# Four of the first eight column blocks of a modulation, moved from VectorE to TensorE as four-byte products

## The chip, the cores and the metric

The kernel runs on one core of one Trainium2 chip. The metric is the time of one execution on the device, in microseconds (us). TensorE multiplies, VectorE and ScalarE (DVE and ACT in the profile) work elementwise, SyncE (SP) issues most of the transfers from memory, GpSimd (POOL) a few. TensorE's weight loads have a row of their own (PEld) and overlap its matmuls (PE).

## The reference, cut to what matters

Two transformer blocks run one after the other on 256 tokens of 1024 features. The first begins so:

```python
mod = c @ w_ada[l] + b_ada[l]                  # c: 1 x 1024, w_ada: 1024 x 3072
shift, scl, gate = jnp.split(mod, 3, axis=-1)
h = rms_norm(x, g_norm[l]) * (1.0 + scl[:, None, :]) + shift[:, None, :]
proj = h @ w_in[l]
```

The change touches `mod` of this first block alone. All values are four-byte floats.

## The kernel before, in words

**The modulation.** The host lays `w_ada` out as 24 column blocks of 128 columns, transposed: block i is a tile of 128 partitions (the columns) x 1024 (the inputs). Shift and scale blocks alternate: block 2k is the shift of features 128k to 128k + 127, block 2k + 1 their scale; the last eight are the gate. `ada` (L368) streams one block into a buffer `raw`, multiplies it with `c1b`, a copy of the condition on every partition, and sums along the row, in one VectorE instruction (L370, with a short read of the accumulator behind it). The result is one column of `mod1`.

**The first projection.** h is kept transposed, in eight blocks of 128 features x 256 tokens, each as two parts, `bh` (rounded) and `bl` (the rest), so that three fast matmuls stand for one exact product (`mm3`, L243 to L246). A loop over kk (L404 to L421) takes four blocks of the modulation at a time, adds the bias (`biased`, L373), forms `am` from the scales (L418) and then two blocks of h (`hT_block`: L330 and L332 on VectorE, L331 on ScalarE). Blocks 8 to 11 and 13 to 15 are each followed by half a projection tile (`proj_n`): its weights are streamed, cast (`whi`, L239, ScalarE), subtracted (`wlo`, L240, VectorE) and used in 24 matmuls of 256 columns. The first tile of weights is called tile 0 in what follows; it needs the first four blocks of h, so blocks 0 to 7.

**Ahead of it** ScalarE squares x, VectorE forms the reciprocal root `rstd` (L289 to L299), and TensorE transposes x in 16 pieces (L319) and spreads `rstd` to rows in a PSUM tile `rb` (L324) that L330 reads.

**What sets the order.** Each engine works its instructions in a fixed order that a scheduler made from the program; the fences below show it. `raw` has five buffers, which blocks and weight tiles share; SP issues a transfer when the buffer's last reader is done, in order. The order holds for whole tiles: a write to any part of a tile waits for its readers so far.

Of the kernel before, what the change touches and what calls it, by code (L numbers as in the profile page):

```python
# [7 lines left out]
F32 = mybir.dt.float32  # L8
# [88 lines left out]
def _pack(I):  # L97
    I = {k: np.asarray(v) for k, v in I.items()}
    A = {}
# [12 lines left out]
    tl = lambda v: v.reshape(-1, 128).T  # L112
# [3 lines left out]
    def inter(w):  # L116

        n = w.shape[-1] // 3072
        w = w.reshape(w.shape[:-1] + (n, 3, 8, 128))
        sc = np.stack([w[..., 0, :, :], w[..., 1, :, :]], axis=-2).reshape(w.shape[:-4] + (n, 2048))  # L120
        return np.concatenate([sc, w[..., 2, :, :].reshape(w.shape[:-4] + (n, 1024))], axis=-1).reshape(w.shape[:-4] + (-1,))
# [5 lines left out]
    A["bcmp"] = np.stack([I["b_cmp_k1_2"][0], I["b_cmp_v1_2"][0]])  # L127
    A["gfin"] = I["g_final"][None]
    A["gnf"] = I["g_norm_final_2"][None]
    A["wada1"] = inter(I["w_ada"][0]).T.reshape(24, 128, 1024)  # L130
    A["wada2"] = inter(I["w_ada_2"][0]).T.reshape(48, 128, 1024)
    w = I["w_in"][0]
    A["win1n"] = rows(cat(w[:, 1024:2560], w[:, 0:512]))
# [4 lines left out]
    w = I["w_in_2"][0]  # L138
# [5 lines left out]
    w = I["w_out_2"][0]  # L144
# [10 lines left out]
    return {k: np.ascontiguousarray(v) for k, v in A.items()}  # L155


VEC = {}
_o = 0
for _n, _w in (("b1", 24), ("g1", 8), ("ps", 4), ("b2", 48), ("gm", 8), ("gf", 8),  # L160
# [10 lines left out]
def _body(ctx, tc, ins, out, dbg, stop):  # L171
    nc = tc.nc
    V, S, G, T = nc.vector, nc.scalar, nc.gpsimd, nc.tensor
# [14 lines left out]
    def vcol(n, i=0, w=None):  # L188
        o, ww = VEC[n]
        return vec[:, o + i:o + i + (ww - i if w is None else w)]  # L190
# [14 lines left out]
    def bc_row(pool, ap, name, tag=None, q=S):  # L205
        t = pool.tile([128, 1024], F32, name=name, tag=tag or name)
        q.dma_start(t, bass.AP(tensor=ap.tensor, offset=ap.offset, ap=[[0, 128], [1, 1024]]))
        return t
# [16 lines left out]
    def stream(name, i):  # L225
        t = raw.tile([128, 1024], F32, name="raw")
        loaded[0] = nc.sync.dma_start(t, ins[name][i])
        return t
# [110 lines left out]
    with ExitStack() as c1:  # L339
        k1 = c1.enter_context(tc.tile_pool(name="k1", bufs=1))  # L340
# [10 lines left out]
        x_sb = k1.tile([128, 2, 1024], F32, name="x_sb")  # L351
        for t in range(2):
            S.dma_start(x_sb[:, t], ins["x"][t * 128:(t + 1) * 128])
        c1b = bc_row(k1, ins["c1"], "c1b", "tm1", nc.sync)
        load_consts(const, "ka")
        ident = K["ident"]
# [12 lines left out]
            for i in range(lo, hi):  # L369
                V.scalar_tensor_tensor(scr2, stream(name, i), 1.0, row, op0=OP.mult, op1=OP.mult, accum_out=mod[:, i:i + 1])  # L370

        def biased(mod, bias, lo, hi):
            V.tensor_add(mod[:, lo:hi], mod[:, lo:hi], vcol(bias, lo, hi - lo))  # L373


        mode[0] = "V"
# [13 lines left out]
        V.tensor_copy(mask, K["mask"])  # L390
        identb = k1.tile([128, 128], BF, name="identb")
        V.tensor_copy(identb, ident)
        rb = pov.tile([128, 256], F32, name="rb", tag="ov")
        for t in range(2):
            rows(rb[:, t * 128:(t + 1) * 128], rstd[:, t:t + 1])
        xT = xT_in(v_sb, u_sb)
# [7 lines left out]
        for kk in range(4):  # L404
            lo = 4 * kk
            for i in range(lo, lo + 4):
                if i > 1:
                    with tc.issue_after(ready.ins):
                        ada("wada1", mod1, c1b, "b1", i, i + 1)
                else:  # L410
                    ada("wada1", mod1, c1b, "b1", i, i + 1)
                for _ in range(begin.get(i, 0)):
                    n = len(first)
                    q, g = ((pmm, "mm"), (pmm, "mm"), (psc, "sc"), (psc, "sc"), (psc, "sc"), (ptr, "tp"), (ptr, "tp"))[n]
                    first.append(q.tile([128, 2, 256], F32, name="mm", tag=g))
                    proj_n(first[n], "win1n", n, *h1, (0,))
            biased(mod1, "b1", lo, lo + 4)
            V.scalar_tensor_tensor(am[:, 2 * kk:2 * kk + 2], mod1[:, lo + 1:lo + 4:2], 1.0, vcol("g1", 2 * kk, 2),  # L418
                                   op0=OP.add, op1=OP.mult)
            for k in (2 * kk, 2 * kk + 1):  # L420
                hT_block(*hT, k, xT, rb, am, lambda k: mod1[:, 2 * k:2 * k + 1], w1)  # L421
# [839 lines left out]
    for c in range(64, 124):  # L1261
        upc(G1, c)
        if c % 4 == 3 and 68 <= c < 100:
            i = 40 + (c - 68) // 4
# [49 lines left out]
```

## Time and profile before

| | us |
|---|---|
| three runs | 1246.6, 1245.26, 1244.03 |
| median | 1245.26 |
| profiled execution, its own time | 1246.62 |
| its span, first to last instruction | 1244.8 |

| stretch (us) | what runs there |
|---|---|
| 0 to 11 | transfers; ScalarE squares x |
| 11 to 16.5 | transposes of x and the rows of rstd on TensorE; VectorE: block 1, rstd, blocks 2 and 3 |
| 16.5 to 24.7 | VectorE: blocks 4 to 8 and the first two blocks of h; TensorE waits |
| 24.7 to 47 | first halves of seven projection tiles; VectorE: blocks 9 to 15, the other blocks of h, the low halves |
| from 47 on | TensorE busy nearly without pause to the end |

The times in the rows below count from the span's start. A timeline row is one instruction, or several like ones in a row (xN); behind it, in brackets, stands how long the engine had been idle and what ended that.

### The profile page before, as it was taken

Reading aid. Unit: us, or ns where it says so; the run is one execution under the profiler, and the core shown is the slowest. Engines: PE = TensorE matmul, PEld = TensorE weight load, DVE = VectorE, ACT = ScalarE, POOL = GpSimd, SP = SyncE. Lnnn points to the kernel's source line nnn. Section 1 sums busy time; section 2 is a strip of 40 time slices with the busy share of each in tenths; the row PEclk is TensorE's granted clock in tenths of the full one; section 3 lists DMA queues with packets and bytes.
Section 4 is the critical chain, followed back from the end, with each engine's and each line's share of the span. In section 5 each row is a group of like instructions: output and inputs, shape, how many; then the busy total and the mean of one; then the engine's idle time right before and its main releaser. Section 6 shows DMA issues by size and latency. Waiting matters only on the chain. (4 is left out here: it accounts for less than half of the span.)

```text
span 1244.8 us, 22791 instructions
## 1 busy us (share of the span) xinstructions
PE 1190.5 (96%) x8960; PEld 1071.1 (86%) x8960; DVE 959.2 (77%) x2015; ACT 585.6 (47%) x907; POOL 8.7 (1%) x14
## 2 busy tenths in 40 slices
PE   3999999899999899899999999999999999999996
PEld 2998899778788799899999999998777777888884
DVE  6879869768798789997546778778888887666555
ACT  3445547323553545454544444445444444555553
POOL 0000000000000000000000000000000000000001
PEclk9999999999999999999999999999999999999998
DMA  9999846287373444556565555555555556777551
GB/s 320 363 323 317 284 163 198 92 287 253 103 238 118 170 143 165 169 171 202 190 195 175 170 170 170 170 169 171 169 172 179 173 172 237 227 230 238 183 186 51
DMA packets 67451, 245.22 MB, mean 197 GB/s; under 512 B 7504, under 2 KB 8032, under 8 KB 67088
## 3 DMA queue, kind: packets, MB, share of 16 engines
q1 hardware_dynamic: 65136, 236.34, 57.7%
q10 hardware_dynamic: 1440, 4.20, 0.9%
q0 software_dynamic: 768, 3.23, 0.8%
q8 instruction: 70, 1.15, 0.4%
q14 instruction: 37, 0.30, 0.1%
HBM read 241.11 MB, written 2.62 MB: 196 GB/s over the span
## 5 line engine op out<-in xcount | busy, mean ns | idle before, releaser
L240 DVE TENSOR_TENSOR wlo<-raw,whi 128x1024 fp32r<-128x1024 f32 x351 | 427.9, 1222 | 121.8 <-ACT whi L239 120.7
L239 ACT CAST whi<-raw 128x1024 fp32r<-128x1024 f32 x351 | 368.0, 1050 | 326.4 <-PE pa L245 221.7
L246 PE MATMUL pa<-bh,wlo 128*128 128x256 f32 x1120 | 314.6, 281 | 3.7 <-DVE wlo L240 3.5
L244 PE MATMUL pa<-bh,whi 128*128 128x256 f32 x1120 | 317.2, 283 | 0.0
L245 PE MATMUL pa<-bl,whi 128*128 128x256 f32 x1120 | 313.9, 280 | 0.0
L246 PEld LDWEIGHTS pa<-bh,wlo 128*128 128x128 f32 x1120 | 211.7, 189 | 5.0 <-DVE wlo L240 4.9
L245 PEld LDWEIGHTS pa<-bl,whi 128*128 128x128 f32 x1120 | 214.5, 192 | 0.0
L244 PEld LDWEIGHTS pa<-bh,whi 128*128 128x128 f32 x1120 | 211.8, 189 | 0.0
L1219 PE MATMUL up<-whi,bh 128*128 128x512 f32 x508 | 164.1, 403 | 0.0
L1219 PE MATMUL up<-wlo,bh 128*128 128x512 f32 x508 | 160.1, 394 | 0.0
L1219 PE MATMUL up<-whi,bl 128*128 128x512 f32 x508 | 159.8, 394 | 0.0
L1219 PEld LDWEIGHTS up<-wlo,bh 128*128 128x128 f32 x508 | 95.4, 188 | 23.5 <-DVE wlo L240 0.3
L1219 PEld LDWEIGHTS up<-whi,bl 128*128 128x128 f32 x508 | 95.4, 188 | 22.3
L244 PE MATMUL mm<-whi,bh 128*128 128x256 f32 x352 | 102.2, 290 | 11.0 <-ACT whi L239 8.2
L1219 PEld LDWEIGHTS up<-whi,bh 128*128 128x128 f32 x508 | 93.4, 189 | 19.3 <-ACT whi L239 0.2
L245 PE MATMUL mm<-wlo,bh 128*128 128x256 f32 x352 | 101.2, 288 | 2.1 <-DVE wlo L240 2.1
L246 PE MATMUL mm<-whi,bl 128*128 128x256 f32 x352 | 101.1, 287 | 1.1 <-DVE bl L332 1.0
L1185 DVE TENSOR_TENSOR RL<-E,wpt 128x512 f16<-128x512 f16 x128 | 53.9, 422 | 33.7 <-PE tp L1199 33.7
L244 PEld LDWEIGHTS mm<-whi,bh 128*128 128x128 f32 x352 | 67.8, 193 | 13.1 <-ACT whi L239 8.6
L245 PEld LDWEIGHTS mm<-wlo,bh 128*128 128x128 f32 x352 | 67.7, 192 | 3.2 <-DVE wlo L240 2.5
L246 PEld LDWEIGHTS mm<-whi,bl 128*128 128x128 f32 x352 | 67.7, 192 | 2.3 <-DVE bl L332 1.7
L231 ACT CAST bh<-Ga 128x256 fp32r<-128x256 f32 x64 | 25.4, 406 | 86.3 <-PE up L1219 85.1
(400 smaller groups left out, 1709.7 us busy)
## 6 DMA issues: line engine op xcount, KB each, us to landing
raw<-in_wdT_dram SPq DMA_DIRECT2D x128, 512.0 KB, 3.4
raw<-in_wu_dram SPq DMA_DIRECT2D x128, 512.0 KB, 3.5
raw<-in_wada_dram SPq DMA_DIRECT2D x72, 512.0 KB, 4.8
raw<-in_win_dram SPq DMA_DIRECT2D x26, 512.0 KB, 4.5
raw<-in_win1t_dram SPq DMA_DIRECT2D x24, 512.0 KB, 5.0
raw<-in_win1n_dram SPq DMA_DIRECT2D x16, 512.0 KB, 5.2
raw<-in_wout_dram SPq DMA_DIRECT2D x16, 512.0 KB, 3.6
raw<-in_wq_dram SPq DMA_DIRECT2D x12, 512.0 KB, 3.6
```

The costliest lines, as they stand in the source:

```text
L231: S.copy(hi, src)
L239: S.copy(hi, t)
L240: (E or eng()).tensor_tensor(lo, t, hi, op=OP.subtract)
L244: T.matmul(o, a[0], b[0], start=first, stop=False, **kw)
L245: T.matmul(o, a[0], b[1], start=False, stop=False, **kw)
L246: T.matmul(o, a[1], b[0], start=False, stop=last, **kw)
L1185: V.tensor_tensor(L[:, p], E, pair(wpt[:, p], t).to_broadcast([128, ng // 2, 64, 2]), op=OP.mult)
L1219: T.matmul(up[t][d], s_[:, ts], v_[:, d], start=ia == 0 and n == 0, stop=ia == 127 and n == 2)
```

## The change

For blocks 0, 2, 4 and 6 (the shifts of the first four blocks of h) the host stores the weights untransposed, as eight pieces of 128 inputs x 128 columns side by side. `ada_t` multiplies each piece, as the stationary operand, with one column of `c1t` (the condition as 128 x 8, a new 4 KB transfer on POOL's queue), and adds the eight products up in one column of PSUM. The four columns lie behind `rb` in the same PSUM tile, now called `rbm`. `biased` adds the bias to the even columns from PSUM and to the odd ones from `mod1`, in two instructions instead of one.

```diff
@@ -127,7 +127,10 @@
     A["bcmp"] = np.stack([I["b_cmp_k1_2"][0], I["b_cmp_v1_2"][0]])
     A["gfin"] = I["g_final"][None]
     A["gnf"] = I["g_norm_final_2"][None]
-    A["wada1"] = inter(I["w_ada"][0]).T.reshape(24, 128, 1024)
+    A["wada1"] = inter(I["w_ada"][0]).T.reshape(24, 128, 1024).copy()
+    for i in ADA_T:
+        A["wada1"][i] = A["wada1"][i].T.reshape(8, 128, 128).transpose(1, 0, 2).reshape(128, 1024)
+    A["c1t"] = tl(I["c"][0])
     A["wada2"] = inter(I["w_ada_2"][0]).T.reshape(48, 128, 1024)
     w = I["w_in"][0]
     A["win1n"] = rows(cat(w[:, 1024:2560], w[:, 0:512]))
@@ -155,6 +158,7 @@
     return {k: np.ascontiguousarray(v) for k, v in A.items()}
 
 
+ADA_T = (0, 2, 4, 6)
 VEC = {}
 _o = 0
 for _n, _w in (("b1", 24), ("g1", 8), ("ps", 4), ("b2", 48), ("gm", 8), ("gf", 8),
@@ -351,6 +355,8 @@
         x_sb = k1.tile([128, 2, 1024], F32, name="x_sb")
         for t in range(2):
             S.dma_start(x_sb[:, t], ins["x"][t * 128:(t + 1) * 128])
+        c1t = k1.tile([128, 8], F32, name="c1t")
+        G.dma_start(c1t, ins["c1t"])
         c1b = bc_row(k1, ins["c1"], "c1b", "tm1", nc.sync)
         load_consts(const, "ka")
         ident = K["ident"]
@@ -369,8 +375,13 @@
             for i in range(lo, hi):
                 V.scalar_tensor_tensor(scr2, stream(name, i), 1.0, row, op0=OP.mult, op1=OP.mult, accum_out=mod[:, i:i + 1])
 
-        def biased(mod, bias, lo, hi):
-            V.tensor_add(mod[:, lo:hi], mod[:, lo:hi], vcol(bias, lo, hi - lo))
+        def ada_t(o, i):
+            w = stream("wada1", i)
+            for k in range(8):
+                T.matmul(o, w[:, k * 128:(k + 1) * 128], c1t[:, k:k + 1], start=k == 0, stop=k == 7, skip_group_check=True)
+
+        def biased(mod, bias, lo, hi, step=1, src=None):
+            V.tensor_add(mod[:, lo:hi:step], mod[:, lo:hi:step] if src is None else src, vcol(bias, lo, hi - lo)[:, ::step])
 
 
         mode[0] = "V"
@@ -390,7 +401,8 @@
         V.tensor_copy(mask, K["mask"])
         identb = k1.tile([128, 128], BF, name="identb")
         V.tensor_copy(identb, ident)
-        rb = pov.tile([128, 256], F32, name="rb", tag="ov")
+        rbm = pov.tile([128, 256 + len(ADA_T)], F32, name="rb", tag="ov")
+        rb, mps = rbm[:, :256], rbm[:, 256:]
         for t in range(2):
             rows(rb[:, t * 128:(t + 1) * 128], rstd[:, t:t + 1])
         xT = xT_in(v_sb, u_sb)
@@ -404,7 +416,9 @@
         for kk in range(4):
             lo = 4 * kk
             for i in range(lo, lo + 4):
-                if i > 1:
+                if i in ADA_T:
+                    ada_t(mps[:, ADA_T.index(i):ADA_T.index(i) + 1], i)
+                elif i > 1:
                     with tc.issue_after(ready.ins):
                         ada("wada1", mod1, c1b, "b1", i, i + 1)
                 else:
@@ -414,7 +428,12 @@
                     q, g = ((pmm, "mm"), (pmm, "mm"), (psc, "sc"), (psc, "sc"), (psc, "sc"), (ptr, "tp"), (ptr, "tp"))[n]
                     first.append(q.tile([128, 2, 256], F32, name="mm", tag=g))
                     proj_n(first[n], "win1n", n, *h1, (0,))
-            biased(mod1, "b1", lo, lo + 4)
+            if lo in ADA_T:
+                n = ADA_T.index(lo)
+                biased(mod1, "b1", lo, lo + 4, 2, mps[:, n:n + 2])
+                biased(mod1, "b1", lo + 1, lo + 4, 2)
+            else:
+                biased(mod1, "b1", lo, lo + 4)
             V.scalar_tensor_tensor(am[:, 2 * kk:2 * kk + 2], mod1[:, lo + 1:lo + 4:2], 1.0, vcol("g1", 2 * kk, 2),
                                    op0=OP.add, op1=OP.mult)
             for k in (2 * kk, 2 * kk + 1):
```

On TensorE, between the last transposes of x (`tp`) and the first matmul of the projection (`mm`), before:

```order
L324 MATMUL rb_137<-ka_103,rstd_110 128x128 [waits DVE_49]
L324 MATMUL rb_137<-ka_103,rstd_110 128x128
L319 MATMUL tp_158<-ka_103,x_sb_98 128x128 [waits Activation_49]
L319 MATMUL tp_158<-ka_103,x_sb_98 128x128 x3
L244 MATMUL mm_214<-whi_217,bh_165 128x256 [waits Activation_49]
L245 MATMUL mm_214<-wlo_218,bh_165 128x256 [waits DVE_49]
```

and after (raw_169, 182, 206 and 219 are blocks 0, 2, 4 and 6; rb_139 is the tile that now holds `rb` and the four columns):

```order
L323 MATMUL tp_160<-ka_105,x_sb_98 128x128 [waits Activation_49]
L323 MATMUL tp_160<-ka_105,x_sb_98 128x128 x3
L381 MATMUL rb_139<-c1t_101,raw_169 128x1 [waits DMAHW2_49,DMASW0_49]
L381 MATMUL rb_139<-c1t_101,raw_169 128x1 x7
L381 MATMUL rb_139<-c1t_101,raw_182 128x1 [waits DMAHW6_49]
L381 MATMUL rb_139<-c1t_101,raw_182 128x1 x7
L381 MATMUL rb_139<-c1t_101,raw_206 128x1 [waits DMAHW1_49,DVE_49]
L381 MATMUL rb_139<-c1t_101,raw_206 128x1 x7
L381 MATMUL rb_139<-c1t_101,raw_219 128x1 [waits DMAHW3_49]
L381 MATMUL rb_139<-c1t_101,raw_219 128x1 x7
L248 MATMUL mm_246<-whi_249,bh_167 128x256 [waits Activation_49]
```

The 32 products stand where TensorE passed straight to the projection, and the third block of them waits for VectorE.

On VectorE, behind the reciprocal root, before (raw_173, 176, 189, 192 and 195 are blocks 2 to 6):

```order
L370 SCALAR_TENSOR_TENSOR scr2_108,mod1_106<-raw_173,c1b_101 128x1024 [waits DMAHW6_49]
L370 SCALAR_TENSOR_TENSOR scr2_108,mod1_106<-raw_176,c1b_101 128x1024 [waits DMAHW0_49,DVE_49]
L373 TENSOR_TENSOR mod1_106<-mod1_106,vec_70 128x4 [waits DMAHW7_49,DVE_49]
L370 SCALAR_TENSOR_TENSOR scr2_108,mod1_106<-raw_189,c1b_101 128x1024 [waits DMAHW1_49]
L418 SCALAR_TENSOR_TENSOR am_164<-mod1_106,vec_70 128x2 [waits DVE_49]
L370 SCALAR_TENSOR_TENSOR scr2_108,mod1_106<-raw_192,c1b_101 128x1024 [waits DMAHW2_49,DVE_49]
L330 SCALAR_TENSOR_TENSOR hT_181<-v_sb_117,am_164,rb_137 128x256 [waits DVE_49,PE_49,Activation_49]
L330 SCALAR_TENSOR_TENSOR hT_185<-v_sb_117,am_164,rb_137 128x256
L370 SCALAR_TENSOR_TENSOR scr2_108,mod1_106<-raw_195,c1b_101 128x1024 [waits DMAHW3_49,DVE_49]
```

and after (raw_192, 216 and 229 are blocks 3, 5 and 7; the two sums that read rb_139 take the even columns):

```order
L376 SCALAR_TENSOR_TENSOR scr2_110,mod1_108<-raw_192,c1b_103 128x1024 [waits DMAHW0_49]
L384 TENSOR_TENSOR mod1_108<-mod1_108,vec_70 128x2 [waits DMAHW7_49,DVE_49]
L437 SCALAR_TENSOR_TENSOR am_166<-mod1_108,vec_70 128x2 [waits DVE_49]
L384 TENSOR_TENSOR mod1_108<-rb_139,vec_70 128x2 [waits PE_49]
L334 SCALAR_TENSOR_TENSOR hT_198<-v_sb_119,am_166,rb_139 128x256 [waits DVE_49,Activation_49]
L334 SCALAR_TENSOR_TENSOR hT_202<-v_sb_119,am_166,rb_139 128x256
L336 SCALAR_TENSOR_TENSOR bl_168<-hT_198,mod1_108,bh_167 128x256 [waits Activation_49]
L376 SCALAR_TENSOR_TENSOR scr2_110,mod1_108<-raw_216,c1b_103 128x1024 [waits DMAHW2_49]
L336 SCALAR_TENSOR_TENSOR bl_168<-hT_202,mod1_108,bh_167 128x256 [waits Activation_49]
L384 TENSOR_TENSOR mod1_108<-rb_139,vec_70 128x2 [waits PE_49]
L376 SCALAR_TENSOR_TENSOR scr2_110,mod1_108<-raw_229,c1b_103 128x1024 [waits DMAHW4_49,DVE_49]
```

VectorE has two waits for TensorE that it had not; block 7 stands behind the second, and behind block 7 come, in this order, its sum and `am`, two L334, block 8, two L336 and the low half of tile 0 (before: block 8, `am`, two L330, the low half, two L332).

On SP's queue, the transfers of blocks 7 and 8 and of the first two projection tiles, before:

```order
L227 DMA raw_198<-in_wada1_dram 128x1024 [waits DMAHW6_49,DVE_49]
L227 DMA raw_211<-in_wada1_dram 128x1024 [waits DMAHW5_49,DMAHW0_49,DVE_49]
L227 DMA raw_215<-in_win1n_dram 128x1024 [waits DMAHW1_49,DVE_49]
L227 DMA raw_245<-in_wada1_dram 128x1024 [waits DMAHW7_49,DMAHW2_49,DVE_49]
L227 DMA raw_249<-in_win1n_dram 128x1024 [waits DMAHW3_49,DVE_49]
```

and after:

```order
L231 DMA raw_229<-in_wada1_dram 128x1024 [waits PE_49]
L231 DMA raw_243<-in_wada1_dram 128x1024 [waits DMAHW6_49,DMAHW5_49,PE_49]
L231 DMA raw_247<-in_win1n_dram 128x1024 [waits DMAHW1_49,PE_49]
L231 DMA raw_277<-in_wada1_dram 128x1024 [waits DMAHW7_49,DMAHW2_49,DVE_49]
L231 DMA raw_281<-in_win1n_dram 128x1024 [waits DMAHW3_49,PE_49]
```

The order of the transfers is the same; four of the buffers now come free by TensorE.

## Rows read from the trace of the kernel before

**Rows 1.** Busy time by stretch: PE, PEld, DVE, ACT, POOL, PEclk, DMA share, GB/s.

```profile
11.00:16.50 5.50, 4.89 (x20) 3.96 (x20) 5.22 (x19) 1.76 (x3) 0.00 (x0) 1.00 1.01 400
16.50:24.70 8.20, 0.07 (x1) 0.00 (x0) 8.13 (x20) 2.51 (x4) 0.00 (x0) 1.00 0.96 299
...
47.00:130.00 83.00, 82.97 (x689) 79.51 (x690) 69.48 (x118) 45.66 (x76) 0.00 (x0) 1.00 0.93 330
```

**Rows 2.** Waits, 0 to 50 us: who for whom, total us, times, longest.

```profile
PE mm L244 <- ACT whi L239: 8.2, 1, 8.2
```

**Rows 3.** Timeline of VectorE: start us, us, engine, line, operation, out<-in.

```profile
14.35 1.22 DVE L370 SCALAR_TENSOR_TENSOR scr<-raw,c1b 128x1024 bf16<-128x1024 f32 x1
...
22.09 1.22 DVE L370 SCALAR_TENSOR_TENSOR scr<-raw,c1b 128x1024 bf16<-128x1024 f32 x1
...
23.36 0.16 DVE L373 TENSOR_TENSOR mod<-mod,vec 128x4 f32<-128x4 f32 x1
23.43 1.22 DVE L370 SCALAR_TENSOR_TENSOR scr<-raw,c1b 128x1024 bf16<-128x1024 f32 x1
...
24.58 0.16 DVE L418 SCALAR_TENSOR_TENSOR am<-mod,vec 128x2 f32<-128x2 f32 x1
24.77 0.87 DVE L330 SCALAR_TENSOR_TENSOR hT<-v_sb,am,rb 128x256 f32<-128x256 f32 x2
25.56 1.22 DVE L240 TENSOR_TENSOR wlo<-raw,whi 128x1024 fp32r<-128x1024 f32 x1
26.69 0.88 DVE L332 SCALAR_TENSOR_TENSOR bl<-hT,mod,bh 128x256 fp32r<-128x256 f32 x2
27.49 1.22 DVE L370 SCALAR_TENSOR_TENSOR scr<-raw,c1b 128x1024 bf16<-128x1024 f32 x1
```

**Rows 4.** Timeline of TensorE's matmuls around the seventh tile.

```profile
46.16 0.28 PE L244 MATMUL mm<-whi,bh 128*128 128x256 f32 x1
47.03 0.39 PE L245 MATMUL mm<-wlo,bh 128*128 128x256 f32 x1 [0.59 <-DVE wlo L240]
```

**Rows 5.** Timeline of TensorE's weight loads, 24 to 33 us.

```profile
24.78 0.29 PEld L244 LDWEIGHTS mm<-whi,bh 128*128 128x128 f32 x1 [8.62 <-ACT whi L239]
26.83 0.29 PEld L245 LDWEIGHTS mm<-wlo,bh 128*128 128x128 f32 x1 [1.76 <-DVE wlo L240]
...
27.43 0.33 PEld L245 LDWEIGHTS mm<-wlo,bh 128*128 128x128 f32 x1
...
31.91 0.33 PEld L245 LDWEIGHTS mm<-wlo,bh 128*128 128x128 f32 x1
...
32.48 0.19 PEld L245 LDWEIGHTS mm<-wlo,bh 128*128 128x128 f32 x1
32.60 0.19 PEld L246 LDWEIGHTS mm<-whi,bl 128*128 128x128 f32 x1
```

**Rows 6.** The same view at three later places.

```profile
280.73 0.32 PEld L801 LDWEIGHTS sc<-gl,wc 128*64 128x64 f32 x8
...
281.63 0.19 PEld L244 LDWEIGHTS mm<-whi,bh 128*128 128x128 f32 x1
...
297.02 1.86 PEld L845 LDWEIGHTS sc<-kcT,nqT 128*128 128x128 f32 x16
```

**Rows 7.** Timelines of TensorE's matmuls (twice, from two starts) and of ScalarE, 15 to 17 us.

```profile
15.51 1.06 PE L319 MATMUL tp<-ka,x_sb 128*128 128x128 f32 x4
...
15.72 0.85 PE L319 MATMUL tp<-ka,x_sb 128*128 128x128 f32 x3
...
16.60 0.59 ACT L320 COPY u_sb<-tp 128x512 f32<-128x512 f32 x1 [1.99 <-PE tp L319]
```

**Rows 8.** Timelines of SP's queue and of ScalarE: the third tile's issue and cast.

```profile
24.69 0.33 SPq L227 DMA_DIRECT2D raw<-in_win1n_dram  x1
...
29.83 1.04 ACT L239 CAST whi<-raw 128x1024 fp32r<-128x1024 f32 x1 [2.54 <-DMA raw<-in_win1n_dram]
```

**Rows 9.** Transfers of the first 20 us: KB each, median us to landing.

```profile
vec<-in_vec_dram ACTq DMA_DIRECT2D x1, 66.0 KB, 10.3
```

## The prediction

> **What bounds the kernel now.** I read the busy time by stretch first, then the waits of the first 50 us, and then the engines' timelines between 14 and 50 us. From 47 to 130 us TensorE is busy 82.97 of 83.00 us [rows 1]. So what happens at the start is simply added: once TensorE is running it does not stop for long, and a start that is x us later ends the kernel x us later. The question is when it gets going, and what holds it until then.
>
> From 16.5 to 24.7 us TensorE does next to nothing, while VectorE is busy 8.13 of 8.20 us [rows 1]; TensorE's wait there is 8.2 us, for the first tile's cast [rows 2]. VectorE is the bound of the start. It forms the column blocks of the modulation, the two factors per block of h, and then the low half of the first weight tile, which lets the projection run at 26.83 [rows 3, 5]. It is still the bound later: at 47.03 TensorE waits 0.59 us for the low half of the seventh tile [rows 4]. The matmul before it began at 46.16 and would have been followed about 0.12 later, so TensorE arrived at 46.28 and lost 0.75 us. What counts is therefore VectorE's chain up to 47 us, with TensorE 0.75 us behind it.
>
> **What the change takes from VectorE.** Blocks 0, 2, 4, 6 leave it. One block costs 1.27 us from its start to the next step (22.09 to 23.36) [rows 3], four of them 5.1 us. Added are two small sums (0.19 each, as from the end of one such step to the next, 24.58 to 24.77). If the work that leaves were hidden on the idle TensorE, the start would come 4.7 us earlier. It isn't free, for two reasons.
>
> **What it adds to TensorE, and where.** Each block is 8 products of a 128x128 four-byte weight tile with one column. A four-byte product stands in the trace as two weight loads and two matmuls: the eight products of line 845 are sixteen loads [rows 6]. So a block is 16 loads with almost no columns behind them, and the load is the price. No row shows a one-column product. The nearest is line 845: the same 128x128 four-byte weights with 32 columns; 16 loads take 1.86 us, of which the last is 0.19, so they are (1.86 - 0.19) / 15 = 0.111 apart [rows 6]. That is at the full clock. At 17 us the engine isn't there: the granted clock is printed as 1.00 for the whole start [rows 1], but the loads of equal matmuls of 256 columns follow each other at 0.213 before 32.3 us (21 steps from 27.43 to 31.91) and at 0.12 after (32.48, 32.60) [rows 5], which are the levels of 1.2 and 2.4 GHz. A load that nothing hinders takes 0.29 at the low level (24.78) [rows 5] and 0.19 at the high one (281.63) [rows 6]: the 0.10 more is what the load itself needs at the high level, so it doubles. I take 0.213 for a load at the low level, 16 x 0.213 = 3.41 us a block; the lower bound is 16 x 0.111 = 1.78 us.
>
> Four blocks are 13.6 us on TensorE. They cannot begin before 16.36: the order puts them behind the last four transposes, which start at 15.51, the second at 15.72 [rows 7], so 0.213 apart: 15.51 + 4 x 0.213. The idle window ahead of the first cast is 8.2 us. And they are not one stream: blocks 4 and 6 write the same PSUM tile that VectorE reads for the factors of h, and the third block waits for a VectorE step; in program order that is the second hT of the first pair, the last reader. VectorE in turn stands at the sum that reads blocks 0 and 2, and again at the one that reads 4 and 6, and everything of its own is queued behind: block 5 and, at the second stop, block 7, the second pair of h, block 8, and the low half of the first tile. This is the opposite of hiding: the products lie on the path.
>
> **The sum,** at the low clock level, in us from the span's start. Hand-over from TensorE to another engine is 0.24 (ACT's copy begins at 16.60 after the array is free at 16.36) [rows 7], from VectorE to TensorE 0.05 (25.56 + 1.22 to 26.83) [rows 3, 5].
> - Array free 16.36; blocks 0 and 2 take 6.82: 23.18. VectorE has done block 3 (it starts at 14.35, as now [rows 3]), the sum of the odd columns and am by about 16, and waits some 7.4 us.
> - Hand-over 0.24, sum 0.19, two hT 0.79 (24.77 to 25.56) [rows 3], hand-over 0.05: 24.45. Blocks 4 and 6: 31.27. Meanwhile VectorE does bl, block 5, bl and waits again, some 5 us.
> - Hand-over 0.24, sum 0.19, block 7 1.27, sum and am 0.38, two hT 0.79, block 8 1.15 (23.43 to 24.58), two bl 0.80 (26.69 to 27.49), low half 1.27 to TensorE's use: 6.09. The projection runs at 37.36.
>
> Before it was 26.83: TensorE is 10.5 us later. VectorE's next step, block 9, starts at 36.09 + 1.13 = 37.22 instead of 27.49, 9.7 us later, because the two bl now stand ahead of the low half instead of behind it. The third tile may cost a little of that: its transfer is issued when block 8 is done and needed 5.14 us from issue to cast before (24.69 to 29.83) [rows 8]; now block 8 ends at 35.29, cast done at 35.29 + 5.14 + 1.04 = 41.47, and VectorE would want it at 37.22 + 3 x 1.14 = 40.64. That is 0.0 to 0.8 more, so VectorE's chain moves by 9.7 to 10.5. TensorE reaches the seventh tile at 46.28 + 10.5 = 56.8, its low half is there at 46.98 + 9.7 to 10.5 = 56.7 to 57.5. The shift is 9.8 to 10.5; I take 10.0.
>
> The transfers don't decide elsewhere. The buffers of blocks 0, 2, 4, 6 now come free by TensorE, so SP issues block 7, block 8 and the first two projection tiles after blocks 0, 2, 4 and 6 of TensorE; the last of these two is issued at about 31.5 and cast by 31.5 + 5.14 + 1.04 = 37.7, before it is needed at 38.4. The first is issued at 28.1, cast at the latest behind the second pair of h. The new transfer of the condition as a column (4 KB, POOL's queue, nothing ahead of it and none behind it at the start) I cost at nothing: even the 66 KB of vec, last in its queue, took 10.3 us to land [rows 9] and was there before 16.36. Were it later than that, every block would wait for it.
>
> The profiled execution takes 1246.62 us; with 10.0 it is 1256.6. The median of the runs is 1.36 lower, 1245.26, so the forecast is 1255.3 us.
>
> **Rivals.** (a) The loads run at 0.111, because the clock rises during the products or because a load doesn't double at the low level. The chain is 23.72 + 4 blocks; with 1.78 it ends at 30.84, TensorE is 4.0 later and VectorE 3.2 to 4.0: 1248.9 us. A rise halfway gives about 1251. For it: TensorE does work without a pause from 16.36 to 23. Against it: 4.89 busy of 5.50 us from 11 to 16.5 [rows 1] didn't raise it, the last transposes still being 0.21 apart [rows 7]; and, for the second reason, the 0.29 against 0.19 of a single load. The Trainium skill, "TensorE: Matmul & The Clock Gate", section "LDWEIGHTS (loading the stationary operand)", gives a load as its columns divided by 1.2 per ns at any clock, 107 ns for 128. By that, as an estimate, the time would be that of this rival; the rows at the high level agree with it (0.111), the single loads at the two levels don't.
>
> (b) Not slower: a load with hardly any columns behind it costs far less than line 845 says. Line 801 shows eight loads of 64 columns with 15 columns moved: 0.32 us in all, the last 0.14, so 0.026 apart [rows 6]. If that held here, a block would be 0.42 us, the chain would end at 25.4, and with VectorE's shift of -2.2 to -1.4 the time would be 1243.8. It turns at (26.83 - 23.72) / 4 = 0.78 us a block, 0.049 a load. Against it: those loads fill half the array, in pairs for two different halves of the output, so four steps of 0.056 explain them, and 128 columns would again be 0.11. The skill's same page, section "Back-to-back issue gap", puts a matmul of 1 to 64 columns at a floor of some 25 ns; by that the blocks would cost 0.4 us each and this rival's time would follow. Its table leaves the loads out; line 845 at 0.111 speaks against it.
>
> (c) Worse: each pass waits until the one before has left the array, since all add to one column: three transposes in a row are busy for 0.85, so one for 0.85 - 2 x 0.213 = 0.42 at the low level [rows 7], 6.7 us a block, 1269 us. Line 801 adds up passes in the same columns at 0.056 and speaks against it.
>
> **How the numbers follow.** Forecast 0.66; (a) with its halfway case 0.21; (b) 0.07; (c) 0.03; anything else 0.03. The range 1248.5 to 1257.5 holds the forecast with its bounds and (a). A measurement of this kernel tells about 0.2% (2.5 us) from no change: slower 0.90, the same 0.07 (most of b), faster 0.03 (b with the projection also finding the full clock).
>
> **What would show it.** After: 64 one-column products from 16.4 us, their loads 0.21 apart; two waits of VectorE for TensorE of about 7 and 5 us at the sums of the even columns; a pause of TensorE of about 5 us ahead of the projection, which runs at 37.4; from 57 us on the old pattern, 10 us later. Wrong would be: loads 0.11 apart or less, a third block that starts right behind the second, or a projection that runs before 31.

## The result, and the profile after

The changed kernel takes 1255.18 us (median of 6 runs, 1253.13 to 1258.19) against 1245.93 for the kernel before, measured beside it (1244.03 to 1250.81). The ratio is 1.0070, 95% interval 1.0046 to 1.0094: the change costs 8.7 us, between 5.7 and 11.7 (the two medians lie 9.25 apart). The forecast was 1255.3.

The profiled execution of the changed kernel takes 1253.13 us, the shortest of its runs; its span is 1251.4 us, against 1244.8 before. The busy time by stretch, in the columns of [rows 1]:

```profile
11.00:16.50 5.50, 4.84 (x30) 4.25 (x30) 4.71 (x20) 2.35 (x4) 0.00 (x0) 1.00 0.80 317
16.50:24.70 8.20, 7.14 (x39) 7.05 (x39) 2.99 (x7) 0.91 (x2) 0.00 (x0) 0.56 0.59 192
47.00:130.00 83.00, 81.56 (x678) 78.45 (x677) 69.92 (x120) 44.89 (x70) 0.00 (x0) 1.00 0.94 332
```

In the middle stretch the two engines have changed places: TensorE, idle before, is busy 7.14 of 8.20 us, and VectorE has gone from 8.13 to 2.99. What VectorE does with the rest is in the waits of the first 60 us (who for whom, total, times, longest):

```profile
DVE mod L384 <- PE rb L381: 9.5, 2, 4.9
...
PE mm L248 <- ACT whi L243: 4.2, 1, 4.2
...
PE mm L249 <- DVE wlo L244: 2.1, 2, 1.1
```

Two waits of VectorE at the sums of the even columns, 9.5 us together, where the kernel before had none. TensorE's own wait ahead of the projection is shorter than in [rows 2] (4.2 against 8.2), which says nothing good: it is filled with products. The timeline of TensorE's matmuls shows where they stand, and how late the projection (L248, L249) is:

```profile
14.54 0.71 PE L328 MATMUL rb<-ka,rstd 128*128 128x128 f32 x4 [0.51 <-DVE rstd L299]
15.09 0.60 PE L323 MATMUL tp<-ka,x_sb 128*128 128x128 f32 x4
15.53 5.09 PE L381 MATMUL rb<-c1t,raw 128*128 128x1 f32 x32
21.67 6.99 PE L381 MATMUL rb<-c1t,raw 128*128 128x1 f32 x32 [1.06 <-DVE hT L334]
32.86 0.58 PE L248 MATMUL mm<-whi,bh 128*128 128x256 f32 x1 [4.20 <-ACT whi L243]
34.45 0.58 PE L249 MATMUL mm<-wlo,bh 128*128 128x256 f32 x1 [1.00 <-DVE wlo L244]
```

The first 32 passes (blocks 0 and 2) take 5.09 us, the second 32 (4 and 6) 6.99, between them the wait of 1.06 for the second `hT`. The projection runs at 34.45 instead of 26.83 [rows 5]. On VectorE's timeline:

```profile
20.65 0.16 DVE L384 TENSOR_TENSOR mod<-rb,vec 128x2 f32<-128x2 f32 x1 [4.63 <-PE rb L381]
...
28.70 0.16 DVE L384 TENSOR_TENSOR mod<-rb,vec 128x2 f32<-128x2 f32 x1 [4.87 <-PE rb L381]
...
33.17 1.22 DVE L244 TENSOR_TENSOR wlo<-raw,whi 128x1024 fp32r<-128x1024 f32 x1
34.30 1.22 DVE L376 SCALAR_TENSOR_TENSOR scr<-raw,c1b 128x1024 bf16<-128x1024 f32 x1
```

The low half of tile 0 starts at 33.17 instead of 25.56, block 9 at 34.30 instead of 27.49 [rows 3]. VectorE has four blocks less to form and is 6.8 us later all the same.

One of the four was no relief to it. Before, VectorE formed block 0 at 8.94 and then waited for the transfer of block 1; without block 0, block 1 starts no earlier. VectorE's timeline before,

```profile
8.94 1.23 DVE L370 SCALAR_TENSOR_TENSOR scr<-raw,c1b 128x1024 bf16<-128x1024 f32 x1 [8.00 <-DMA raw<-in_wada_dram]
...
10.83 1.23 DVE L370 SCALAR_TENSOR_TENSOR scr<-raw,c1b 128x1024 bf16<-128x1024 f32 x1 [0.66 <-DMA raw<-in_wada_dram]
```

and after:

```profile
10.88 1.23 DVE L376 SCALAR_TENSOR_TENSOR scr<-raw,c1b 128x1024 bf16<-128x1024 f32 x1 [9.95 <-DMA raw<-in_wada_dram]
```

**Why the first 32 passes are the shorter.** In this execution TensorE was at its upper level, 2.4 GHz, when it came to them. The weight loads, from two starts:

```profile
15.42 2.12 PEld L381 LDWEIGHTS rb<-c1t,raw 128*128 128x128 f32 x18
...
17.31 3.21 PEld L381 LDWEIGHTS rb<-c1t,raw 128*128 128x128 f32 x15
```

Up to 17.3 us they are 0.111 apart ((17.31 - 15.42) / 17), from then on 0.213 (3.21 / 15). They are 0.111 apart at line 845 too, at the upper level. The busy time by stretch has the granted clock, the third column from the right, before and after that:

```profile
14.10:17.40 3.30, 2.86 (x26) 2.86 (x26) 1.81 (x7) 1.14 (x2) 0.00 (x0) 1.00 0.59 199
17.50:22.00 4.50, 3.44 (x17) 3.35 (x17) 1.16 (x4) 0.74 (x2) 0.00 (x0) 0.50 0.63 198
```

The second row ties 0.213 to a granted clock of 0.50, which is 1.2 GHz. The 1.00 of the first row would prove little by itself: near the start it is also printed where the loads are 0.213 apart (e8, below), so there I read the level from the spacing of the loads. This one execution shows both prices of a load.

### The profile page after: what moved, and what is told of

Read it like the earlier page. It is cut to its first block, busy times and chain, and to the rows that moved or that the text cites. A ratio compares the mean times of both kernels' runs of the same rounds, so it can differ in the third digit from the quotient of the medians.

```text
span 1251.4 us, 22916 instructions
## 1 busy us (share of the span) xinstructions
PE 1199.3 (96%) x9024; PEld 1079.7 (86%) x9024; DVE 954.3 (76%) x2009; ACT 587.3 (47%) x907; POOL 9.2 (1%) x15
## 5 line engine op out<-in xcount | busy, mean ns | idle before, releaser
L248 PE MATMUL pa<-bh,whi 128*128 128x256 f32 x1120 | 316.5, 283 | 0.0
L249 PE MATMUL pa<-bl,whi 128*128 128x256 f32 x1120 | 313.4, 280 | 0.0
L249 PEld LDWEIGHTS pa<-bl,whi 128*128 128x128 f32 x1120 | 214.0, 191 | 0.0
L248 PEld LDWEIGHTS pa<-bh,whi 128*128 128x128 f32 x1120 | 211.4, 189 | 0.0
L248 PE MATMUL mm<-whi,bh 128*128 128x256 f32 x352 | 101.5, 288 | 7.3 <-ACT whi L243 4.2
L249 PE MATMUL mm<-wlo,bh 128*128 128x256 f32 x352 | 100.7, 286 | 2.1 <-DVE wlo L244 2.1
L248 PEld LDWEIGHTS mm<-whi,bh 128*128 128x128 f32 x352 | 66.9, 190 | 9.1 <-ACT whi L243 4.3
L249 PEld LDWEIGHTS mm<-wlo,bh 128*128 128x128 f32 x352 | 67.0, 190 | 3.4 <-DVE wlo L244 2.6
```

Source lines behind the costliest of these rows:

```text
L248: T.matmul(o, a[0], b[0], start=first, stop=False, **kw)
L249: T.matmul(o, a[0], b[1], start=False, stop=False, **kw)
```

## The experiments

To compare traces I use one row that all have: the spread of the second root (`rb<-ka,r`, L324 or L328) near 212 us, behind the first projection and a pause of TensorE of 1.3 us. In the kernel before and the changed one it is:

```profile
211.94 0.49 PE L324 MATMUL rb<-ka,r 128*128 128x128 f32 x2 [1.30 <-DVE r L295]
```

```profile
219.67 0.49 PE L328 MATMUL rb<-ka,r 128*128 128x128 f32 x2 [1.32 <-DVE r L299]
```

All runs in one table. A time is the median of a run; the line of before spans the medians that were measured beside the runs (1245.93, 1246.9 and 1247.66, and a single execution of 1248.75). Each ratio is to the one beside it, so ratios compare better than times. "Projection" is the first matmul with the low half of tile 0; "loads" is how far apart the loads of the products were in the trace.

| run | time, us | ratio to before (95%) | projection | row near 212 | loads |
|---|---|---|---|---|---|
| before, first trace | 1245.9 to 1248.8 | 1 | 26.83 | 211.94 | |
| changed | 1255.18 | 1.0070 (1.0046 to 1.0094) | 34.45 | 219.67 | 0.111, then 0.213 |
| e8, changed again | 1255.49 | one run | 37.15 | 221.75 | 0.213 |
| e1, products nobody reads | 1251.62 | 1.0034 (1.0023 to 1.0045) | 32.97 | 217.64 | 0.213 |
| e2, half the products | 1247.88 | 1.0003 (0.9989 to 1.0016) | 30.25 | 214.71 | 0.213 |
| e3, 64 columns | 1253.19 | 1.0037 (1.0020 to 1.0054) | 35.09 | 220.14 | 0.213 |
| e4, own tiles | 1249.84 | 1.0022 (1.0006 to 1.0038) | 32.86 | 216.87 | 0.213 |
| e5, nobody reads, held | 1248.71 | 1.0002 (0.9991 to 1.0013) | 30.28 | 214.41 | 0.213 |
| e6, own tiles, held | 1253.54 | 1.0040 (1.0025 to 1.0055) | 32.75 | 217.96 | 0.111, then 0.213 |
| e7, block 6 only | 1245.58 | 0.9989 (0.9972 to 1.0005) | 26.77 | 212.55 | 0.213 |
| e9, before again | 1248.86 | one run | 26.77 | 212.49 | |
| e10, before again | 1248.86 | one run | 26.84 | 213.39 | |
| e11, e5 again | 1248.15 | one run | 27.17 | 211.57 | 0.111, then 0.213 |

**The theory:** the loads of the products have a price set by the clock, and they lie on the path because VectorE stands still for them. The rivals: TensorE's time counts whoever waits; the two stops with their hand-overs count, not the loads; the shared PSUM tile counts; the columns count. One slip runs through the expectations of e1, e2, e3 and e5: they count 128 loads or 128 passes for the 32 products, where it is 64. Their times for the loads (13.6 us, 6.8 us, 30.0 us) are those of 64; only rival 1 of e3 doubles with it, its 6.8 us should read 3.4.

### The same kernel at the lower clock (e8)

> The changed kernel once more, for a second look at its trace. Theory (two levels of the clock explain the spread of the runs): if the products run wholly at the lower level, each stop takes 6.8 us, the projection runs at 37.4 us, and TensorE is 10 us later than before at 130 us; if the clock is up for part of them as in the first trace, 34.5 us and 8.3 us later. What the end of the kernel shows beyond that comes from the short drops of the clock later on, which differ from run to run.

This execution had the products wholly at the lower level, by their spacing (6.83 us for 32). TensorE's matmuls:

```profile
16.49 6.83 PE L381 MATMUL rb<-c1t,raw 128*128 128x1 f32 x32
24.37 6.99 PE L381 MATMUL rb<-c1t,raw 128*128 128x1 f32 x32 [1.06 <-DVE hT L334]
...
37.15 0.58 PE L249 MATMUL mm<-wlo,bh 128*128 128x256 f32 x1 [1.01 <-DVE wlo L244]
```

and VectorE:

```profile
23.35 0.16 DVE L384 TENSOR_TENSOR mod<-rb,vec 128x2 f32<-128x2 f32 x1 [7.25 <-PE rb L381]
...
31.40 0.16 DVE L384 TENSOR_TENSOR mod<-rb,vec 128x2 f32<-128x2 f32 x1 [4.87 <-PE rb L381]
...
37.01 1.22 DVE L376 SCALAR_TENSOR_TENSOR scr<-raw,c1b 128x1024 bf16<-128x1024 f32 x1
```

Every step of the forecast stands here in its place, within 0.3 us: products 16.49 (16.36 forecast), third block 24.37 (24.45), projection 37.15 (37.36), waits 7.25 and 4.87 (7.4 and 5), block 9 at 37.01 (37.22). TensorE is 9.8 us late at the row near 212. The granted clock is printed as 1.00 all the same; the busy time of the stretch of the first products:

```profile
16.50:23.30 6.80, 6.80 (x33) 6.73 (x32) 0.00 (x0) 0.58 (x1) 0.00 (x0) 1.00 0.47 154
```

### Half of the products (e2)

```diff
-            for k in range(8):
+            for k in range(4):
```

> The changed kernel with four of the eight products in each of the four columns; the other half of each sum is left out. Theory (the weight loads are the price, and they lie on the path): 64 loads fewer; at 0.213 each that is 13.6 / 2 = 6.8 us less, 1255.2 - 6.8 = 1248.4 us, at 0.111 it is 3.6 us less, 1251.6. VectorE's two waits for TensorE shrink by 3.4 us each. Rival (the price is the two stops themselves, their hand-overs and the order of VectorE's work, whatever the length of the products): less than 2 us less, 1253 or more.

```profile
16.43 3.41 PE L381 MATMUL rb<-c1t,raw 128*128 128x1 f32 x16
20.89 3.58 PE L381 MATMUL rb<-c1t,raw 128*128 128x1 f32 x16 [1.06 <-DVE hT L334]
...
30.25 0.58 PE L249 MATMUL mm<-wlo,bh 128*128 128x256 f32 x1 [1.01 <-DVE wlo L244]
```

These are TensorE's matmuls. Each row of products is 3.41 or 3.42 us shorter, what 16 loads at 0.213 are; VectorE's two waits shrink by 3.41 each, from 7.25 and 4.87 in e8 to 3.84 and 1.46. The projection is 6.9 earlier than in e8 (37.15 - 30.25), the row near 212 7.0 (221.75 - 214.71); 6.8 was expected. The time falls to 1247.88 (1248.4 expected) and can't be told from before. Both stops with their hand-overs are still there, so the rival's 1253 or more should stand here; it doesn't, and the loads are the price.

### 64 columns in place of one (e3)

```diff
-                T.matmul(o, w[:, k * 128:(k + 1) * 128], c1t[:, k:k + 1], start=k == 0, stop=k == 7, skip_group_check=True)
+                T.matmul(o, w[:, k * 128:(k + 1) * 128], c1t[:, k:k + 1].to_broadcast([128, 64]), start=k == 0, stop=k == 7, skip_group_check=True)
...
-        rbm = pov.tile([128, 256 + len(ADA_T)], F32, name="rb", tag="ov")
+        rbm = pov.tile([128, 512], F32, name="rb", tag="ov")
```

> The changed kernel with the column of the condition repeated 64 times as the moving side, so that each pass moves 64 columns through the array where it moved one; VectorE reads the first of them. Theory (the load is the price of a pass, columns hide behind it): the loads stay as far apart as with one column, 0.213 at the lower clock level and 0.111 at the upper, and at equal clock the time stays 1255. Rival 1 (a pass costs its load and its columns): 64 columns at 1.2 GHz are 0.053 us, over 64 passes of a stop and 64 of the other 6.8 us more, 1262. Rival 2 (the clock fell during the products because they moved one column only, and stays up with 64): loads 0.111 apart throughout, 64 x 0.1 us less on each of the two stops against the lower level, 1249.

```profile
16.43 6.93 PE L381 MATMUL rb<-c1t,raw 128*128 128x64 f32 x32
```

TensorE's 32 passes with 64 columns take 6.93 us against 6.83 with one. The weight loads of the first row, in e3 and in e8:

```profile
16.22 6.95 PEld L381 LDWEIGHTS rb<-c1t,raw 128*128 128x128 f32 x32
```

```profile
16.28 6.95 PEld L381 LDWEIGHTS rb<-c1t,raw 128*128 128x128 f32 x32
```

The loads are as far apart as with one column; the 0.10 comes once in a row of products and not with each pass. The columns hide behind the loads, and rival 1 (columns count) falls. Rival 2 isn't seen: the clock was at the lower level before the products began here, so this run can't say whether columns would have kept it up. The time is 2 us below the changed kernel (4 by the ratios) and not equal to it. The larger tile also changed VectorE's order: block 7 (1.27) now stands ahead of the second stop, the two `bl` (0.80) behind the low half. That is 2.07, and the projection is 2.06 earlier than in e8 (35.09 against 37.15), the row near 212 1.6.

### Products that nobody reads (e1, e5, e11)

```diff
+        idle = psc.tile([128, 4], F32, name="idle", tag="sc")
+        for i in range(4):
+            for k in range(8):
+                T.matmul(idle[:, i:i + 1], x_sb[:, 0, k * 128:(k + 1) * 128], c1t[:, k:k + 1], start=k == 0, stop=k == 7, skip_group_check=True)
```

in the kernel before, behind the transposes in the text.

> The kernel before, with 32 products added behind the last transposes: four columns of eight, as in the change, with pieces of x as weights, in a PSUM tile of their own. Nobody reads them; VectorE forms all blocks itself, so no engine waits for a product. Theory (VectorE's two stops carry the loss, TensorE's own time little of it): the products run from 16.4 us, 128 loads at 0.213, to 30.0; the projection starts 3.2 us later than 26.8, VectorE is not delayed, and of the 3.2 us the 0.75 that TensorE waited at the seventh tile are given back: 1245.9 + 2.4 = 1248.3 us. Should the clock be at its upper level for all of them, they end at 23.5 and nothing changes, 1245.9. Rival (a product costs what TensorE spends on it, whoever waits): 9 to 10 us more, 1255.

This run missed what it was for. The products had no input that arrives late, so the order put them first, and TensorE's matmuls show them ahead of the transposes:

```profile
7.70 13.81 PE L405 MATMUL idle<-c1t,x_sb 128*128 128x1 f32 x64 [7.70 <-DMA c1t<-in_c1t_dram]
21.37 3.58 PE L320 MATMUL tp<-ka,x_sb 128*128 128x128 f32 x16
```

The transposes, which begin at 11.11 in the kernel before, came at 21.37, and VectorE stood at its first `hT`:

```profile
25.50 0.87 DVE L331 SCALAR_TENSOR_TENSOR hT<-v_sb,am,rb 128x256 f32<-128x256 f32 x2 [5.96 <-ACT u_sb L321]
```

It does show that the 64 passes cost 4.2 us (2.9 to 5.6) if they stand ahead of something that VectorE needs. e5 is the run that was meant, the products held behind the last transposes:

> The kernel before with 32 products that nobody reads, like the run e1_nobody, but held behind the last transposes, where the changed kernel has its own (in e1 the order had put them ahead of the transposes, which then came 9 us late). VectorE forms all blocks itself. Theory (what costs is that VectorE stands still for the products): 128 loads at 0.213 from 16.4 to 30.1 us; the projection runs 3.2 us later than 26.8, VectorE's steps stay where they were, 0.75 of the 3.2 is given back at the seventh tile: 1246.9 + 2.4 = 1249.3 us at the lower clock level, 1246.9 at the upper. Rival (TensorE's time for the products is the cost, whoever waits): 1255.

```profile
16.41 13.65 PE L406 MATMUL idle<-c1t,x_sb 128*128 128x1 f32 x64
29.92 0.56 PE L245 MATMUL mm<-whi,bh 128*128 128x256 f32 x1
30.28 0.41 PE L246 MATMUL mm<-wlo,bh 128*128 128x256 f32 x1
```

and on VectorE, the low half of tile 0:

```profile
25.61 1.22 DVE L241 TENSOR_TENSOR wlo<-raw,whi 128x1024 fp32r<-128x1024 f32 x1
```

The same 64 loads at the same price, and the time is 0.2 us longer (-1.1 to 1.6). VectorE's steps stay (25.61 against 25.56 before). The rival (whoever waits) is out: 1255 lies far outside. The theory's 2.4 us were too many as well. A second trace shows a likely reason:

> The products that nobody reads, held behind the transposes, once more. Theory A: if the clock is up during the products, they take 7.1 to 13.6 us and TensorE is at most 2.5 us later than in the traces of before at the row near 212 us. Theory B: 2.5 us later than in each trace of before again, and what is gained behind it follows the number of drops.

```profile
15.55 11.40 PE L406 MATMUL idle<-c1t,x_sb 128*128 128x1 f32 x64
26.81 0.56 PE L245 MATMUL mm<-whi,bh 128*128 128x256 f32 x1
```

Here the clock was up at first, the products were done about when VectorE's low half was, and TensorE reached the row near 212 at 211.57, no later than before. How often the executions behind the median are of the one kind or the other isn't known. Either way, hardly any of the 8.7 us is TensorE's time as such: it is VectorE's standing still.

### The shared PSUM tile (e4, e6)

The columns of blocks 0 and 2, and of 4 and 6, in two tiles of their own:

```diff
-        rbm = pov.tile([128, 256 + len(ADA_T)], F32, name="rb", tag="ov")
-        rb, mps = rbm[:, :256], rbm[:, 256:]
+        rb = pov.tile([128, 256], F32, name="rb", tag="ov")
+        mps = [psc.tile([128, 2], F32, name="mps", tag="sc") for _ in range(2)]
```

> The changed kernel with the columns in two PSUM tiles of their own (blocks 0 and 2 in one, 4 and 6 in the other) in place of the tile that rb is in. The order of the program changes with it: TensorE now has block 0 ahead of the first transposes and most of block 2 between them, and block 4 no longer waits for the second hT; VectorE has the sum for blocks 0 and 2 in the middle of the reciprocal root. Theory (the shared tile held the products back to 16.4 us and stopped the third block): block 0 takes 8.2 to 11.6 us, block 2 about 14.3 to 18.6, VectorE stops in the root until 18.8, blocks 4 and 6 run from 20.4 to 27.2, the projection starts at 33 and the time is 1251.5 us at the lower clock level; at the upper one blocks 4 and 6 are done by 20.4, before VectorE asks, and the time is 1246. Rival (the tile costs only the one wait of 1.1 us that the changed kernel's trace shows): 1254.

```profile
9.04 3.54 PE L381 MATMUL mps<-c1t,raw 128*128 128x1 f32 x16 [9.04 <-DMA raw<-in_wada_dram]
...
14.18 2.99 PE L381 MATMUL mps<-c1t,raw 128*128 128x1 f32 x14
...
20.25 6.83 PE L381 MATMUL mps<-c1t,raw 128*128 128x1 f32 x32
...
32.86 0.58 PE L249 MATMUL mm<-wlo,bh 128*128 128x256 f32 x1 [1.01 <-DVE wlo L244]
```

TensorE's matmuls stand nearly as expected (projection 32.86 against 33), and the time is 1249.84 (1251.5 expected), 5 us better than the change: block 0 now runs in TensorE's idle time ahead of the transposes, most of block 2 between them. It is still slower than before. e6 asks what of this is the tile's wait and what the order's:

> Like e4_own_tiles (columns in two PSUM tiles of their own), but with all 32 products held behind the last transposes as in the changed kernel, so that only the wait of the third block for the second hT is gone. Theory (this wait lies on the path, but is all that the shared tile costs once the order is fixed): one stretch of products from 16.4 to 30.1 us, the second stop of VectorE ends 1.2 us earlier than in the changed kernel, the projection runs at 36.1 against 37.4 and the time is 1.2 us less, 1254. Rival (the shared tile is the cause of the loss): 1247 to 1250, as e4_own_tiles.

```profile
15.59 11.38 PE L382 MATMUL mps<-c1t,raw 128*128 128x1 f32 x64
...
32.75 0.58 PE L249 MATMUL mm<-wlo,bh 128*128 128x256 f32 x1 [1.01 <-DVE wlo L244]
```

One stretch, no wait at the third block. The trace is of the same kind as the first of the changed kernel (upper level first, then lower), and against that the projection is 1.7 us earlier (34.45 - 32.75), the row near 212 too (219.67 - 217.96): the wait of 1.06 is gone, and the clock fell some 0.6 us later. The time, 1253.54, is 1.6 below the changed kernel's median, and the intervals of the two ratios overlap.

e4 had its products wholly at the lower level, so against e6 the traces need an estimate. At that level e6's products would run from 16.49 (e8) for 13.65 us (e5), and its projection stands 5.78 behind their end (32.75 - 15.59 - 11.38): 35.9. By that the wait that the shared tile brings is worth 1.2 us of the projection (37.15 in e8), and that the order held all products back behind the transposes 3.1 (35.9 - 32.86). The times fall in the same order, 1.0070, 1.0040 and 1.0022, but neighbouring intervals overlap: they don't show which of the two steps is the larger.

### One block only (e7)

> Only block 6 on TensorE, in a PSUM tile of its own; VectorE forms the other seven of the first eight. Theory (a block's loads cost nothing as long as VectorE has other work until they are done): its 16 loads run from about 17 us (its transfer lands at 16.8) to 20.4, VectorE asks for it at 20.8 or later and doesn't stop; the first tile's low half could begin 1.1 us earlier than 25.56, but its cast ends at 24.72, so 0.8 is gained at most: 1246 us, no change that can be told. Rival (each block on TensorE costs its loads): 3.4 less 1.3, 1249.

```profile
17.71 3.54 PE L381 MATMUL mps<-c1t,raw 128*128 128x1 f32 x16 [1.90 <-DMA raw<-in_wada_dram]
...
26.77 0.58 PE L249 MATMUL mm<-wlo,bh 128*128 128x256 f32 x1 [2.03 <-DVE wlo L244]
```

The cost is gone with the other three blocks, as expected; the gain isn't there either. TensorE waited for the block's transfer until 17.71, and so VectorE stopped after all:

```profile
21.30 0.16 DVE L384 TENSOR_TENSOR mod<-mps,vec 128x1 f32<-128x1 f32 x1 [0.81 <-PE mps L381]
```

0.81 of the 1.1 us that it had saved went there, the rest into the two further sums; the projection runs at 26.77. The ratio, 0.9989 (0.9972 to 1.0005), doesn't tell it from the kernel before, and no version here is faster than that one beyond its interval.

### How far executions of one kernel differ (e9, e10)

> The kernel before once more, for its trace. In the traces so far the changed kernel and its variants reach the rows L324/L328 near 212 us (the spread of the second norm's root, behind a pause of TensorE of 1.3 us) later than the first trace of before by 1 to 3.6 us more than their times are longer: 2.5 us for the products that nobody reads, whose time is hardly longer at all. Theory A (executions differ at the start: the clock rises at one moment or another, and the first trace of before had an early one): this trace reaches that row at 213 to 215 us, not at 211.9, with the clock rising later than 32.4. Theory B (executions differ behind it: short drops of the clock between 220 and 530 us, three in the first trace of before, none to three in the others): it reaches the row at 211.9 within 0.3, and its end differs by 1 to 1.7 us for each drop more or fewer than three.

> The same again, a third trace of the kernel before: theory A 213 to 215 us at the row near 212, theory B 211.9 within 0.3 and an end that follows the number of drops.

The row near 212 stands at 212.49 and 213.39: one a little, one clearly later than 211.94, so neither theory alone holds. In e9 the clock even rose earlier, at 29.7 us, and it gained nothing: TensorE then waited for VectorE's low halves four times, 3.2 us in all, against twice and 2.1 us in the first trace. Behind that row the clock drops for a few us at places that vary: a stretch of the first trace of before, and one of e5,

```profile
227.00:230.00 3.00, 3.00 (x16) 3.00 (x15) 1.86 (x6) 0.98 (x4) 0.00 (x0) 0.50 0.02 5
```

```profile
213.00:434.00 221.00, 205.07 (x1471) 171.53 (x1470) 174.49 (x516) 97.08 (x223) 1.06 (x2) 1.00 0.54 180
```

with 0.50 at 227 us in the one and no drop from 213 to 434 in the other. Both executions take 1248.86 us, 2.2 more than the one that the forecast was worked out on; of e10's, 1.45 was there at the row near 212, of e9's 0.55. What brought each drop about I didn't test.

## Why the prediction was right, step by step

- **VectorE bounds the start.** Shown by e5: the same products, with nobody waiting for them, cost 0.2 us (-1.1 to 1.6). An earlier rise of the clock didn't help TensorE either (e9).
- **Four blocks leave VectorE, 5.1 us.** Too much by one block: block 0 ran in time that VectorE had to spare, so three blocks count, 3.8 us. From 14.35 to block 9 at 27.49 VectorE works 13.1 us before, with hardly a pause; in e8 it is 22.5 us from 14.49 to 37.01, of which 12.3 are waits, so 10.2 of work. That is 2.9 us less; the added sums and the steps beside them took the rest. The 4.7 us that hiding the products was to gain were not there to be had. The forecast doesn't suffer from it, because its sum adds VectorE's steps one by one from 16.36 on (block 9 at 37.01, forecast 37.22).
- **A block is 16 loads, the load is the price, 0.213 at the lower level.** Shown by e2 (half the loads, 6.9 us), e3 (32 loads take 6.95 us with 64 columns as with one) and e8 (6.83 for 32 passes, 6.82 forecast). The prices of rival (b), 0.026 a load, and rival (c), 0.42 a pass, appear in no trace. Of rival (a) a part is real: the lower bound, 0.111, holds for the first 17 loads of the first trace. On this the Trainium skill, "TensorE: Matmul & The Clock Gate", section "LDWEIGHTS (loading the stationary operand)", gives a load as its columns divided by 1.2 per ns, 107 ns for 128, and names no clock with it. At the upper level the rows agree (0.111), at the lower they don't (0.213); by that figure e8 would, as an estimate, have had its projection at about 30.4 (37.15 less 64 x 0.106).
- **It can't begin before 16.36.** 16.49 at the lower level; 15.53 where the clock was up during the last transposes too, a case that I had not priced.
- **The third block waits for the second `hT`.** Right, 1.06 us in both traces, and without it the projection is 1.7 us earlier (e6, 0.6 of it by the clock).
- **The sum.** At the lower level right in each line (e8), up to the seventh tile: its low half starts at 55.48 against 45.76 before, 9.7 us later, where 9.7 to 10.5 was forecast. The case of a rise "halfway" was the wrong way round: in the first trace the clock was up at the start and fell. With two blocks at each price it gives 34.1 for the projection (23.72 + 2 x 3.41 + 2 x 1.78), and so about 1252 us, not 1251. That the first trace has 34.45 is luck: it began 0.8 us earlier and had 17 of its 64 loads at the upper price, not half.
- **From the shift to the time.** This term is weaker than the 0.1 us between forecast and median looks. The shift of 10.0 was added to one execution of before, which reaches the row near 212 at 211.94; the mean of the three traces is 212.6. Against that mean the changed kernel is 9.1 us late in e8 and 7.1 in the first trace, 8.1 on average, and the measured loss is 8.7 (5.7 to 11.7). So, as far as two traces and the medians tell, 10.0 was one to two us too many, because some executions have the clock up, and the runs of before measured beside the change were 0.7 above those that the forecast started from. The two errors partly cancel: the mechanism was right and its size nearly so, and the agreement within 0.1 us is luck.
- **Transfers don't decide.** Right up to the projection; behind it, not wholly. In the first trace of the changed kernel VectorE stood for the transfer of block 11, and TensorE then for the low half of the fifth tile (a row of VectorE, then one of TensorE):

```profile
40.62 1.23 DVE L376 SCALAR_TENSOR_TENSOR scr<-raw,c1b 128x1024 bf16<-128x1024 f32 x1 [1.53 <-DMA raw<-in_wada_dram]
```

```profile
48.70 0.38 PE L249 MATMUL mm<-wlo,bh 128*128 128x256 f32 x1 [1.09 <-DVE wlo L244]
```

In e8 VectorE's wait there is 0.37, and TensorE doesn't wait. What this cost the first execution in the end I didn't test. In e7 a transfer decided too: the block's own came after TensorE was free.

## What to carry to other kernels

Moved work pays only if it ends before the engine that was relieved asks for it: here 13.6 us of loads went into an idle window of 8.2, and the bound engine waited. Count as relief only work that the bound engine does while it is bound; a block that it forms while it would wait for a transfer anyway is none. Price a product with few columns by its weight loads, at the clock that TensorE has at that place, and look in the order for what else the moved work now stands in front of or behind. A run with the work done but nobody waiting for it separates an engine's occupancy from the waits on it.

## What the runs showed of the hardware beside that

- The granted clock fell from 2.4 to 1.2 GHz at 17.4 us in the first trace, while TensorE did nothing but one-column products, without a pause, from 15.53 on; in e11 and e6, again with products on end, at about 18. In e7 it fell at about 17.6, while TensorE stood idle from its last transpose to 17.71. In e8 and e5 the clock was low when the products began (loads 0.213 apart from the first on), and 6.8 to 13.7 us of them did not raise it. It rose during the 256-column matmuls of the projection (in e8 they follow each other at 0.21 at 42.86 and at 0.12 from 43.23).
- Executions of one program differ in whether the clock is up at 14 us: in the first trace, e6, e7 and e11 the four steps of `rb` take 0.71 to 0.75 us, in the others 1.22, or 0.61 in e1, where they come at 24.79. The projection of the changed kernel stands 2.7 us apart in its two traces, of which 0.1 is a later start of the whole.
- The profile prints a granted clock of 1.00 at the start of every trace, also where the loads are 0.213 apart (e8, 16.5 to 23.3 us). Where a change is printed, the loads go with it (0.50 and 0.213 in the first trace of the changed kernel).
- A four-byte pass of a 128x128 weight tile costs its load alone, with one column as with 64: 32 loads take 6.95 us in both.
